# VectorE's order around a block of projections: the short convolution behind the background's taps, and root mean squares computed early

## The chip, the cores and the metric

The kernel runs on one core of a Trainium2 chip. The metric is the device time of one execution in microseconds (us), the median of a few runs. The engines are TensorE (PE in the profile; PEld is its weight load), VectorE (DVE), ScalarE (ACT), GpSimd (POOL) and SyncE (SP), which only issues DMAs here.

## What is computed

One layer of an encoder, for two requests (g = 0 and g = 1) of 2048 tokens with 1024 channels. All weights are shared.

```
h = rmsnorm(x, norm_g);  p = h @ w_in                      # 1024 -> 3328 columns
hy_u, hy_z, cf_a, cf_z, xa_q, xa_z = split(p)
u  = depthwise_conv(hy_u, width 3) -> x0, x1, v
y_hy = x0 * fftconv(v * x1, k2, skip) * silu(hy_z)         # k2: a filter from a small MLP
y_cf = silu(layernorm(depthwise_conv(val * sigmoid(gate), width 31))) * silu(cf_z)
y_xa = attention(xa_q, rmsnorm(mem)) * silu(xa_z)
out  = rmsnorm(x + concat(y_hy, y_cf, y_xa) @ w_out, final_g)
```

## The kernel before

The kernel has three stages. Stage 1 (0 to about 1350 us) makes the projection h @ w_in. Stage 2 (to about 1690 us) runs attention and the frequency side of the long convolution. Stage 3 makes the output projection. The change touches stage 1 only.

In stage 1 the loop goes over the 26 columns of 128 outputs of request 0, then over those of request 1, and in each column over four token tiles `tb` of 512. One column and one token tile are called a **block** here. A block is 24 matmuls of 128x512 (`proj`, L502 to L504) into a PSUM tile `pj`, of which there are two. What follows depends on the column: `x1`, `v` and `x0` are the inputs of the width-3 convolution (`hy_conv`), `z` is a gate that ScalarE writes (L568), `cf` columns feed the width-31 convolution, `q` and `zx` go to attention.

`hy_conv` (L509) takes two tiles of the pool `sm` (six buffers): GpSimd copies the 65 last elements of the tile before (L515), ScalarE copies the PSUM tile (L516, this frees `pj`), GpSimd makes the middle tap (L523), VectorE adds the two others (L525, L527), and in `v` and `x0` columns GpSimd multiplies the result into a 2048-wide tile of the pool `big` (`gate`, L544; three buffers). The finished `big` tile is written to DRAM at the column's end; for `v` columns ScalarE issues that DMA (L558).

Beside the blocks runs **background** work, kept in two queues `fq` and `bgq` of pieces (cost, chain, function). After each block `background(us)` gives a credit of 5.4 us less the block's own VectorE cost (2.2 for x0, x1 and v, 0.8 for cv and q, 0.1 otherwise), and runs pieces until the credit is used. A piece marked as chain runs only when its queue has run nothing yet in that block. The pieces that matter here:

- `cf_background`: the width-31 convolution of one request: four token tiles of 512 tokens, two halves of channels, 30 taps each, each one VectorE instruction (L276, cost 0.9). When both halves are done there follows a chain of five steps: `total` (GpSimd adds, L282), `center` (TensorE means, L286, then VectorE subtracts, L292), `squares`, `var` (L286 again, ScalarE's root, VectorE's reciprocal, L302) and `outp`. The next token tile's first 31 pieces are spread between these steps in five parts.
- `filter_background` (request 1): a three-layer MLP with a sine (L358 on VectorE, L361 and L362 on GpSimd, L364 three times on VectorE, L365), and the filter's taps (L389, L390).
- `kv_background` and `a_background`: keys and values, and the first part of stage 2.

Where request 0 ends, `load_x` loads and normalizes the tokens of request 1 (`normed`): four row tiles of 256 KB per 256 tokens for the sum of squares (L436, ScalarE's L437), and the same tokens transposed in two DMAs of 512 KB (L439) that VectorE scales (L449) by a row that TensorE broadcasts (L447). `build_xt` splits the result into two halves `xh` and `xl` (L468, L469).

The order of each engine's instructions is made by a scheduler when the kernel is built: from the source, it takes what its own timing says is ready. `in_order` binds chosen engines to the source's order: each instruction of a background piece stands behind the one that the source has before it on that engine. It binds TensorE and ScalarE.

Of the kernel before, what the change touches and what calls it, by code (L numbers as in the profile page):

```python
# [18 lines left out]
P = 128  # L19
L = 2048  # L20
D = 1024
# [86 lines left out]
def kernel(ctx: ExitStack, tc: tile.TileContext, a: dict):  # L108
# [77 lines left out]
    def background(us):  # L186

        pace["block"] += 1
        pace["credit"] = min(pace["credit"], us) + us
        chained = set()  # L190
        while pace["credit"] > 0:
            for q in (fq, bgq):
                if not q:
                    continue
                cost, chain, fn = q[0]
                if chain and (id(q) in chained or pace["last"][id(q)] == pace["block"]):
                    continue
                if chain:
                    chained.add(id(q))
                q.popleft()  # L200
                with in_order():
                    fn()
                pace["last"][id(q)] = pace["block"]
                pace["credit"] -= cost
                break
            else:
                break
# [37 lines left out]
    with ExitStack() as c1:  # L245
# [20 lines left out]
        def cf_background(g):  # L266
# [54 lines left out]
            for b in range(NB + 1):  # L321
                first = list(half(sts[b], b, 0)) if b < NB else []
                n = -(-len(first) // 5)
                for i in range(5):
                    bgq.extend(chain[i:i + 1])
                    bgq.extend(first[i * n:(i + 1) * n])
                if b < NB:
                    bgq.extend(half(sts[b], b, 1))
                chain = [(us, True, lambda f=f, b=b: f(sts[b], b)) for us, f in (
                    (0.0, total), (1.4, center), (0.0, squares), (3.4, var), (0.0, outp))]  # L330
# [120 lines left out]

        def load_x(g, tb, mid=None):
            xn = []
            for h in range(2):
                if h and mid:
                    mid()
                xn.append(big().rearrange("p (k t) -> p k t", k=KC))
                normed(xn[h], a["xt"][g, tb, h], xs[g][0, tb * TB + h * 256:tb * TB + (h + 1) * 256, :], 0)
            return xn
# [49 lines left out]
        def hy_conv(st, ps, ch, tb, dst=None):  # L509
# [7 lines left out]
            if tb == NB - 1:  # L517
# [6 lines left out]
                                    op0=ALU.mult, op1=ALU.add)  # L524
            nc.vector.scalar_tensor_tensor(ct[:, o:e], pt[:, o:e], w[0], ct[:, o:e], op0=ALU.mult, op1=ALU.add)  # L525
# [3 lines left out]
            return out, o, e  # L529
# [17 lines left out]
        def hy_u(g, i):  # L547
            st = {}

            def x1(tb, ps):  # L550
                if tb == 0:
                    st["u"] = big()
                hy_conv(st, ps, 4 + i, tb, st["u"])

            def v(tb, ps):
                gate(st["u"], tb, hy_conv(st, ps, 8 + i, tb))
                if tb == NB - 1:
                    nc.scalar.dma_start(UU[i].rearrange("c (n g t) -> c n g t", g=2, t=32)[:, :, g, :],  # L558
                                        st["u"].rearrange("p (n t) -> p n t", t=32))
            return [(COL_X1 + i * P, x1), (COL_V + i * P, v)]  # L560

        def hy_g(g, i):
# [7 lines left out]
            def x0(tb, ps):  # L570
                gate(st["u"], tb, hy_conv(st, ps, i, tb))
                if tb == NB - 1:
                    perm_out(st["u"], GG, i, g)
# [119 lines left out]
        def a_background(n0):  # L693
# [20 lines left out]
            def mult(i):  # L714
# [3 lines left out]
                for s in range(2):  # L718
# [10 lines left out]
        QUEUE = {(0, 0): [kv_background], (0, 4): [lambda: cf_background(0)], (1, 0): [filter_background],  # L729
                 (1, 4): [lambda: cf_background(1)],  # L730
# [31 lines left out]
        for idx, (g, n_, cs) in enumerate(seq):  # L762
            if n_ == 0:
                n = 0
            if True:
# [7 lines left out]
                for tb in range(NB):  # L773
# [3 lines left out]
                    for w, (_, f) in zip(ws, cs):  # L777
                        f(tb, proj(w, tb, 256 if first and tb < HB else TB))
# [333 lines left out]
```

## Time and profile before

| | us |
|---|---|
| median of 3 runs | 2106.33 (2104.52 to 2107.66) |
| profiled execution | 2107.82 |
| its span, first to last instruction | 2106.0 |

The profiled execution is 1.5 us above the median. PE has records for 94% of the span, at a mean granted clock of 0.977 of full speed; DVE is busy for 59%, ACT for 37%, POOL for 40%. In the views "idle before" names what ended an engine's idle time, and `x` counts instructions.

### The profile page before, as it was taken

How to read it: one execution, taken by the hardware profiler on the slowest of the kernel's cores; microseconds unless marked ns; L12 is line 12 of the kernel's file. 1: busy time of each engine (PE TensorE's matmuls, PEld its weight loads, DVE VectorE, ACT ScalarE, POOL GpSimd, SP SyncE). 2: the span in 40 equal slices, each digit the busy share in tenths (PEclk: the TensorE clock that was granted, in tenths of full speed). 3: DMA queues.
4: the chain of work that ended last, by engine and by line, in shares of the span. 5: the costliest groups of instructions: out<-in, count | busy, mean ns of one | idle time of the engine just before them, and what ended most of it. 6: DMA issues, size and time to landing. Idle time of an engine off the chain costs nothing. (4 is left out here: it accounts for less than half of the span.)

```text
span 2106.0 us, 25970 instructions
## 1 busy us (share of the span) xinstructions
PE 1983.5 (94%) x8866; PEld 1500.1 (71%) x8866; DVE 1233.5 (59%) x1779; ACT 780.4 (37%) x1468; POOL 847.8 (40%) x838
## 2 busy tenths in 40 slices
PE   5999989998998999999998999899988899999998
PEld 5887778777887787777776877777533267777776
DVE  4533974959646379445448865278887624344443
ACT  4422112131335244444431222278688622222221
POOL 3332766554543222344434441266598711111110
PEclk8999999999999999999999999999999999999999
DMA  9634134342458323233341325698888685555552
GB/s 333 210 106 158 68 93 116 99 133 80 171 191 278 131 86 108 82 96 84 102 116 56 118 88 189 221 291 263 245 273 273 215 218 135 152 159 148 152 145 61
DMA packets 238558, 328.72 MB, mean 156 GB/s; under 512 B 87177, under 2 KB 117913, under 8 KB 236634
## 3 DMA queue, kind: packets, MB, share of 16 engines
q1 hardware_dynamic: 146026, 260.72, 38.9%
q10 hardware_dynamic: 87056, 54.57, 9.6%
q0 software_dynamic: 5344, 11.77, 2.0%
q8 instruction: 71, 1.16, 0.2%
q14 instruction: 61, 0.50, 0.1%
HBM read 196.37 MB, written 130.61 MB: 155 GB/s over the span
## 5 line engine op out<-in xcount | busy, mean ns | idle before, releaser
L502 PE MATMUL pj<-xh,whi 128*128 128x512 f32 (+1 forms) x1728 | 679.0, 393 | 23.6 <-ACT xh L468 6.7
L503 PE MATMUL pj<-xl,whi 128*128 128x512 f32 (+1 forms) x1728 | 673.4, 390 | 9.7 <-POOL xl L469 9.7
L504 PE MATMUL pj<-xh,wlo 128*128 128x512 f32 (+1 forms) x1728 | 671.8, 389 | 2.0 <-POOL wlo L235 2.0
L276 DVE SCALAR_TENSOR_TENSOR bg<-bg,vb,bg 128x512 f32<-128x512 f32 x480 | 399.0, 877 | 39.6 <-POOL bg L271 35.7
L502 PEld LDWEIGHTS pj<-xh,whi 128*128 128x128 f32 x1728 | 332.3, 193 | 105.2 <-ACT sm L516 15.0
L503 PEld LDWEIGHTS pj<-xl,whi 128*128 128x128 f32 x1728 | 332.8, 193 | 79.7 <-POOL xl L469 11.0
L504 PEld LDWEIGHTS pj<-xh,wlo 128*128 128x128 f32 x1728 | 332.5, 192 | 71.0 <-issue 3.6
L1057 PE MATMUL ms<-wo,mh 128*128 128x512 f32 x512 | 204.3, 399 | 2.2 <-ACT mh L234 2.2
L1058 PE MATMUL ms<-wo,mh 128*128 128x512 f32 x512 | 201.2, 393 | 0.0
L1059 PE MATMUL ms<-wo,ml 128*128 128x512 f32 x512 | 194.3, 397 | 0.2 <-POOL ml L235 0.2
L516 ACT COPY sm<-pj 128x512 f32<-128x512 f32 x96 | 56.5, 589 | 353.4 <-PE pj L504 272.0
L525 DVE SCALAR_TENSOR_TENSOR sm<-sm,va,sm 128x448 f32<-128x448 f32 (+1 forms) x96 | 77.7, 809 | 145.5 <-POOL sm L523 106.0
L544 POOL TENSOR_TENSOR big<-big,sm 128x448 f32<-128x448 f32 (+1 forms) x64 | 121.2, 1894 | 100.9 <-DVE sm L527 100.9
L1060 DVE TENSOR_TENSOR xr<-xr,ms 128x512 f32<-128x512 f32 x64 | 44.0, 688 | 199.0 <-PE ms L1059 198.9
L523 POOL TENSOR_SCALAR sm<-sm,va 128x448 f32<-128x448 f32 (+1 forms) x96 | 110.9, 1155 | 114.3 <-ACT sm L516 110.6
L241 POOL TENSOR_TENSOR ss<-ss,mhalf 128x1 f32<-128x1 f32 x32 | 17.7, 553 | 313.3 <-DVE ss L240 313.3
L1057 PEld LDWEIGHTS ms<-wo,mh 128*128 128x128 f32 x512 | 96.9, 189 | 47.4 <-issue 24.3
L1059 PEld LDWEIGHTS ms<-wo,ml 128*128 128x128 f32 x512 | 96.5, 188 | 21.0 <-DVE mf L1043 0.8
L1058 PEld LDWEIGHTS ms<-wo,mh 128*128 128x128 f32 x512 | 96.9, 189 | 20.0
L239 ACT ACTIVATE junk<-xr 128x1024 bf16<-128x1024 f32 x32 | 33.9, 1060 | 192.4 <-DVE xr L1060 185.9
L925 POOL TENSOR_TENSOR z<-z,us 128x512 f32<-128x512 f32 x64 | 81.9, 1289 | 31.3 <-DVE us L924 22.7
L235 POOL TENSOR_TENSOR wlo<-sm,whi 128x512 fp32r<-128x512 f32 x50 | 75.6, 1526 | 37.2 <-ACT whi L234 28.9
(169 smaller groups left out, 2758.6 us busy)
## 6 DMA issues: line engine op xcount, KB each, us to landing
big<-in_xt_dram SPq DMA_DIRECT2D x32, 512.0 KB, 6.8
in<-x1d SPq DMA_DIRECT2D x128, 128.0 KB, 3.6
aa<-o ACTq DMA_DIRECT2D x64, 256.0 KB, 3.5
at<-aa SPq DMA_DIRECT2D x64, 256.0 KB, 5.0
out_dram<-xr ACTq DMA_DIRECT2D x64, 256.0 KB, 3.8
sm<-in_win_dram SPq DMA_DIRECT2D x52, 256.0 KB, 3.6
ws<-whi SPq DMA_DIRECT2D x52, 256.0 KB, 3.0
ws<-wlo SPq DMA_DIRECT2D x52, 256.0 KB, 4.2
```

The source lines that it names most:

```text
L235: (sub_eng or nc.gpsimd).tensor_tensor(lo, src, hi.bitcast(F32), op=ALU.subtract)
L276: nc.vector.scalar_tensor_tensor(st["a", c], st["h", c][:, k:k + TB], vb[:, 2 * k + c:2 * k + c + 1], st["a", c], op0=ALU.mult, op1=ALU.add)
L502: nc.tensor.matmul(ps[:, ts_], hi, xh[:, k, ts_], start=k == 0, stop=False)
L503: nc.tensor.matmul(ps[:, ts_], hi, xl[:, k, ts_], start=False, stop=False)
L504: nc.tensor.matmul(ps[:, ts_], lo, xh[:, k, ts_], start=False, stop=k == KC - 1)
L523: nc.gpsimd.tensor_scalar(ct[:, o:e], pt[:, o + 1:e + 1], w[1], va[:, 52 + ch:53 + ch], op0=ALU.mult, op1=ALU.add)
L525: nc.vector.scalar_tensor_tensor(ct[:, o:e], pt[:, o:e], w[0], ct[:, o:e], op0=ALU.mult, op1=ALU.add)
L544: nc.gpsimd.tensor_tensor(v, v, out, op=ALU.mult)
L925: nc.gpsimd.tensor_tensor(z, z, us, op=op)
L1057: nc.tensor.matmul(po, mh[:, k, :], woh[k][:, hs], start=i == 0, stop=False)
L1058: nc.tensor.matmul(po, mh[:, k, :], wol[k][:, hs], start=False, stop=False)
L1059: nc.tensor.matmul(po, ml[:, k, :], woh[k][:, hs], start=False, stop=i == 7)
```

## The change

- `in_order` around a background piece binds VectorE too.
- `hy_conv` becomes a generator: up to GpSimd's middle tap it runs where it did; VectorE's two instructions and the gate (`later`) run after the block's background call, bound to VectorE's source order.
- Credit that a block does not use lapses (before, up to one block's worth was kept).
- The chain of `cf_background` has eight steps, three of them empty; the next tile's pieces are spread between them in eight parts.
- The sums of squares of request 1 are made by a background of their own (`squares_background`) during columns v(1) to x1(3) of request 0: eight loads of 1 MB each into `big` tiles, two ScalarE instructions each, the results kept in `rs1`. `load_x` of request 1 (`normed_known`) then has no row loads and no squares.
- Request 1's `cf_background` is queued one column earlier.

```diff
-        pace["credit"] = min(pace["credit"], us) + us
+        pace["credit"] = min(pace["credit"], 0.0) + us
...
-                with in_order():
+                with in_order((nc.tensor, nc.scalar, nc.vector)):
                     fn()
...
-                n = -(-len(first) // 5)
-                for i in range(5):
+                n = -(-len(first) // 8)
+                for i in range(8):
...
-                    (0.0, total), (1.4, center), (0.0, squares), (3.4, var), (0.0, outp))]
+                    (0.0, None), (0.0, total), (1.4, center), (0.0, None), (0.0, squares), (0.0, None), (3.4, var), (0.0, outp))]
...
+        def squares_background():
...
+            def rows_in(i):
+                st[i] = big().rearrange("p (j d) -> p j d", j=2)
+                nc.sync.dma_start(st[i], xs[1][0, i * 256:(i + 1) * 256, :].rearrange("(j p) d -> p j d", p=P))
...
+            def rstd(i):
+                t, ss = st.pop(i), rs1[:, 2 * i:2 * i + 2]
+                for j in range(2):
+                    nc.scalar.activation(t[:, j, :], t[:, j, :], AF.Square, accum_out=ss[:, j:j + 1])
+                nc.vector.tensor_scalar(ss, ss, 1.0 / D / 65536, EPS / 65536, op0=ALU.mult, op1=ALU.add)
+                nc.gpsimd.tensor_tensor(ss, ss, mhalf.broadcast_to([P, 2]), op=ALU.pow)
...
+            for i in range(8):
+                fq.append((0.0, True, lambda i=i: rows_in(i)))
+                fq.append((0.2, True, lambda i=i: rstd(i)))
...
+        def normed_known(xb, src, i):
...
+            for k in range(0, KC, 4):
+                nc.sync.dma_start(xb[:, k:k + 4, :], src[:, k:k + 4, :])
+            dg, r = bt(), ms()[:, 0:256]
+            for t in range(2):
+                dt = dg[:, t * P:(t + 1) * P]
+                nc.vector.tensor_scalar(dt, ident, rs1[:, 2 * i + t:2 * i + t + 1], None, op0=ALU.mult)
+                nc.tensor.matmul(r[:, t * P:(t + 1) * P], ones.bitcast(F32), dt, start=True, stop=True)
...
                                     op0=ALU.mult, op1=ALU.add)
+            yield
             nc.vector.scalar_tensor_tensor(ct[:, o:e], pt[:, o:e], w[0], ct[:, o:e], op0=ALU.mult, op1=ALU.add)
...
             def v(tb, ps):
-                gate(st["u"], tb, hy_conv(st, ps, 8 + i, tb))
-                if tb == NB - 1:
+                cv = hy_conv(st, ps, 8 + i, tb)
+                next(cv)
+
+                def rest():
+                    gate(st["u"], tb, next(cv))
...
-        QUEUE = {(0, 0): [kv_background], (0, 4): [lambda: cf_background(0)], (1, 0): [filter_background],
-                 (1, 4): [lambda: cf_background(1)],
+        QUEUE = {(0, 0): [kv_background], (0, 7): [squares_background], (0, 4): [lambda: cf_background(0)], (1, 0): [filter_background],
+                 (1, 3): [lambda: cf_background(1)],
...
-                    for w, (_, f) in zip(ws, cs):
-                        f(tb, proj(w, tb, 256 if first and tb < HB else TB))
+                    later = [f(tb, proj(w, tb, 256 if first and tb < HB else TB)) for w, (_, f) in zip(ws, cs)]
...
                         background(sum(5.4 - own(col) for col, _ in cs))
+                    with in_order((nc.vector,)):
+                        for f in later:
+                            if f:
+                                f()
```

What this does to VectorE's order is seen at three places. The first is the first x1 column of request 0. Before, 28 taps (L276) stand ahead of the first convolution instruction; the last of them and the first block's convolution (L525, L527; tile `big` is its result) are:

```order
L276 SCALAR_TENSOR_TENSOR bg_2055<-bg_2053,vb,bg_2055 128x512
L525 SCALAR_TENSOR_TENSOR sm_1752<-sm_1749,va,sm_1752 128x448
L276 SCALAR_TENSOR_TENSOR bg_1758<-bg_1756,vb,bg_1758 128x512
L276 SCALAR_TENSOR_TENSOR bg_2419<-bg_2417,vb,bg_2419 128x512
L276 SCALAR_TENSOR_TENSOR bg_2055<-bg_2053,vb,bg_2055 128x512
L527 SCALAR_TENSOR_TENSOR big_1748<-sm_1749,va,sm_1752 128x7x64
L525 SCALAR_TENSOR_TENSOR sm_1800<-sm_1797,va,sm_1800 128x512
L276 SCALAR_TENSOR_TENSOR bg_1758<-bg_1756,vb,bg_1758 128x512
L276 SCALAR_TENSOR_TENSOR bg_2419<-bg_2417,vb,bg_2419 128x512
```

After the change the same column, from its first tap on (L563 and L565 are the convolution now):

```order
L276 SCALAR_TENSOR_TENSOR bg_1757<-bg_1755,vb,bg_1757 128x512 x4
L563 SCALAR_TENSOR_TENSOR sm_1753<-sm_1750,va,sm_1753 128x448
L565 SCALAR_TENSOR_TENSOR big_1749<-sm_1750,va,sm_1753 128x7x64
L276 SCALAR_TENSOR_TENSOR bg_1757<-bg_1755,vb,bg_1757 128x512 x4
L563 SCALAR_TENSOR_TENSOR sm_1797<-sm_1794,va,sm_1797 128x512
L565 SCALAR_TENSOR_TENSOR big_1749<-sm_1794,va,sm_1797 128x8x64
L276 SCALAR_TENSOR_TENSOR bg_1757<-bg_1755,vb,bg_1757 128x512 x3
```

The taps of three half tiles no longer run ahead of the convolution; each block has its three or four taps, then its convolution. The second place is VectorE around the third token tile's `center` (L292) in request 0, before:

```order
L525 SCALAR_TENSOR_TENSOR sm_3690<-sm_3686,va,sm_3690 128x576
L276 SCALAR_TENSOR_TENSOR bg_3451<-bg_3449,vb,bg_3451 128x512
L276 SCALAR_TENSOR_TENSOR bg_3727<-bg_3725,vb,bg_3727 128x512
L527 SCALAR_TENSOR_TENSOR sm_3690<-sm_3686,va,sm_3690 128x576
...
L276 SCALAR_TENSOR_TENSOR bg_3451<-bg_3449,vb,bg_3451 128x512
L276 SCALAR_TENSOR_TENSOR bg_3727<-bg_3725,vb,bg_3727 128x512 x4
L292 TENSOR_TENSOR bg_3163<-bg_3163,ms_3765 128x512
L292 TENSOR_TENSOR bg_3451<-bg_3451,ms_3765 128x512
```

and after:

```order
L276 SCALAR_TENSOR_TENSOR bg_3631<-bg_3629,vb,bg_3631 128x512 x22
L276 SCALAR_TENSOR_TENSOR bg_3899<-bg_3897,vb,bg_3899 128x512 x3
L563 SCALAR_TENSOR_TENSOR sm_3895<-sm_3892,va,sm_3895 128x448
L565 SCALAR_TENSOR_TENSOR sm_3895<-sm_3892,va,sm_3895 128x448
L276 SCALAR_TENSOR_TENSOR bg_3899<-bg_3897,vb,bg_3899 128x512 x4
L563 SCALAR_TENSOR_TENSOR sm_3939<-sm_3936,va,sm_3939 128x512
L565 SCALAR_TENSOR_TENSOR sm_3939<-sm_3936,va,sm_3939 128x512
L292 TENSOR_TENSOR bg_3267<-bg_3267,ms_3991 128x512
L292 TENSOR_TENSOR bg_3631<-bg_3631,ms_3991 128x512
```

Before, the last tap of the half tile that is centered (`bg_3451`) stands four taps ahead of `center`, at the end of a run in which every other tap is one of the next tile (`bg_3727`); after, two convolutions and seven taps of the next tile stand between them. The third place is VectorE in the `x1` and `v` columns of request 1, where the filter's MLP runs beside the blocks. Before, the convolutions of several blocks stand between the filter's steps, and the scheduler fills the gaps:

```order
L358 TENSOR_SCALAR f_6376<-ms_6374,va 128x256
L390 TENSOR_TENSOR f_6371<-ms_6367,f_6371 128x512
L525 SCALAR_TENSOR_TENSOR sm_6363<-sm_6359,va,sm_6363 128x576
L364 SCALAR_TENSOR_TENSOR f_6376<-f_6280,f_6376 128x256
L527 SCALAR_TENSOR_TENSOR big_6209<-sm_6359,va,sm_6363 128x9x64
L364 SCALAR_TENSOR_TENSOR f_6376<-f_6280,f_6376 128x256 x2
```

After, L364 (which waits for GpSimd's L362) stands directly behind L358, and the taps and the convolution behind both:

```order
L390 TENSOR_TENSOR f_7355<-ms_7351,f_7355 128x512
L358 TENSOR_SCALAR f_7362<-ms_7360,va 128x256
L364 SCALAR_TENSOR_TENSOR f_7362<-f_7358,f_7362 128x256 x3
L276 SCALAR_TENSOR_TENSOR bg_6847<-bg_6845,vb,bg_6847 128x512
L563 SCALAR_TENSOR_TENSOR sm_7347<-sm_7343,va,sm_7347 128x576
L565 SCALAR_TENSOR_TENSOR sm_7347<-sm_7343,va,sm_7347 128x576
```

Nothing else can be taken in the time that L364 waits.

## Rows read from the trace of the kernel before

**Rows 1.** Windows of stage 1: length, busy us and (x instructions) by engine, PEclk, DMA.

```profile
260.00:285.00 25.00, 19.03 (x72) 15.18 (x71) 25.00 (x29) 2.81 (x5) 17.15 (x13) 0.86 0.45 105
400.00:420.00 20.00, 15.01 (x58) 11.88 (x57) 20.00 (x23) 2.99 (x4) 9.23 (x6) 0.83 0.34 68
420.00:440.00 20.00, 17.80 (x70) 13.89 (x69) 16.71 (x24) 4.61 (x7) 7.38 (x8) 0.91 0.28 81
440.00:510.00 70.00, 70.00 (x309) 57.57 (x308) 48.17 (x53) 18.23 (x24) 42.51 (x34) 1.00 0.31 107
510.00:540.00 30.00, 23.31 (x88) 17.76 (x87) 23.23 (x29) 7.17 (x10) 10.66 (x10) 0.83 0.30 109
635.00:705.00 70.00, 60.90 (x259) 48.92 (x258) 47.11 (x91) 35.32 (x67) 27.20 (x18) 0.93 0.80 263
705.00:1125.00 420.00, 420.00 (x1874) 330.08 (x1873) 234.26 (x344) 171.94 (x228) 143.10 (x204) 1.00 0.31 92
1125.00:1150.00 25.00, 17.77 (x68) 13.52 (x68) 18.38 (x26) 4.72 (x6) 6.80 (x7) 0.86 0.24 79
1210.00:1235.00 25.00, 20.12 (x76) 15.17 (x75) 15.51 (x18) 4.96 (x7) 7.31 (x4) 0.86 0.23 81
```

**Rows 2.** Waits of PE, 200 to 1345 us: us in total, times, longest.

```profile
PE ms L286 <- POOL bg L282: 21.0, 4, 7.2
PE pj L502 <- ACT sm L516: 6.6, 2, 6.0
PE ms L447 <- DVE bg L446: 5.3, 2, 3.8
PE pj L502 <- ACT big L568: 5.0, 1, 5.0
PE pj L502 <- DVE sm L610: 3.8, 3, 2.4
```

**Rows 3.** Timeline of DVE, 505 to 530 us: start, us, line, count.

```profile
506.40 21.55 DVE L276 SCALAR_TENSOR_TENSOR bg<-bg,vb,bg 128x512 f32<-128x512 f32 x25
```

**Rows 4.** Timelines of ACT and POOL, 246 to 276 us.

```profile
271.47 0.60 ACTq L558 DMA_DIRECT2D uu<-big  x1
272.19 0.59 ACT L516 COPY sm<-pj 128x512 f32<-128x512 f32 x1 [15.45 <-POOL sm L515]
...
269.29 2.16 POOL L544 TENSOR_TENSOR big<-big,sm 128x576 f32<-128x576 f32 x1 [3.40 <-DVE sm L527]
```

**Rows 5.** Costliest groups of DVE, 200 to 640 us: busy, mean ns, idle before.

```profile
L276 DVE SCALAR_TENSOR_TENSOR bg<-bg,vb,bg 128x512 f32<-128x512 f32 x233 | 203.4, 922 | 18.8 <-POOL bg L271 16.8 <-POOL sm L513 0.7
L525 DVE SCALAR_TENSOR_TENSOR sm<-sm,va,sm 128x512 f32<-128x512 f32 (+2 forms) x48 | 41.8, 871 | 72.4 <-POOL sm L523 56.1 <-POOL sm L513 16.3
L527 DVE SCALAR_TENSOR_TENSOR sm<-sm,va,sm 128x512 f32<-128x512 f32 (+2 forms) x32 | 31.1, 971 | 0.6
L527 DVE SCALAR_TENSOR_TENSOR big<-sm,va,sm 128x512 f32<-128x512 f32 (+2 forms) x16 | 22.4, 1399 | 0.2
```

**Rows 6.** Costliest groups of POOL on the page, whole span.

```profile
L544 POOL TENSOR_TENSOR big<-big,sm 128x448 f32<-128x448 f32 (+1 forms) x64 | 121.2, 1894 | 100.9 <-DVE sm L527 100.9
L523 POOL TENSOR_SCALAR sm<-sm,va 128x448 f32<-128x448 f32 (+1 forms) x96 | 110.9, 1155 | 114.3 <-ACT sm L516 110.6
```

**Rows 7.** The group of ACT nearest to the new squares, whole span.

```profile
L239 ACT ACTIVATE junk<-xr 128x1024 bf16<-128x1024 f32 x32 | 33.9, 1060 | 192.4 <-DVE xr L1060 185.9 <-DMA xr<-in_x_prompt_dram 6.3 <-DMA g<-gg 0.2
```

**Rows 8.** DMA issues on the page: KB each, median us to landing.

```profile
big<-in_xt_dram SPq DMA_DIRECT2D x32, 512.0 KB, 6.8
```

**Rows 9.** Groups of DVE beside the filter, 900 to 1100 us.

```profile
L364 DVE SCALAR_TENSOR_TENSOR f<-f,f 128x256 f32<-128x256 f32 x33 | 18.8, 570 | 11.4 <-POOL f L362 10.7
L390 DVE TENSOR_TENSOR f<-ms,f 128x512 f32<-128x512 f32 x18 | 12.4, 691 | 37.5 <-ACT f L389 36.9 <-PE ms L387 0.5
L358 DVE TENSOR_SCALAR f<-ms,va 128x256 f32<-128x256 f32 x11 | 5.9, 536 | 5.3 <-PE ms L356 5.3
```

**Rows 10.** The tap's group on DVE at 226 to 248 us, then at 248 to 282 us.

```profile
L276 DVE SCALAR_TENSOR_TENSOR bg<-bg,vb,bg 128x512 f32<-128x512 f32 x22 | 16.2, 786 | 0.0
L276 DVE SCALAR_TENSOR_TENSOR bg<-bg,vb,bg 128x512 f32<-128x512 f32 x25 | 26.2, 1097 | 0.0
```

**Rows 11.** Window of the column v(0).

```profile
226.00:248.00 22.00, 22.00 (x98) 18.09 (x97) 20.98 (x30) 3.40 (x6) 12.42 (x9) 1.00 0.13 48
```

More of the change, by code (lines that the diff above doesn't have):

```diff
@@ L328, in cf_background @@
                     bgq.extend(half(sts[b], b, 1))
-                chain = [(us, True, lambda f=f, b=b: f(sts[b], b)) for us, f in (
-                    (0.0, total), (1.4, center), (0.0, squares), (3.4, var), (0.0, outp))]
+                chain = [(us, True, lambda f=f, b=b: f and f(sts[b], b)) for us, f in (
+                    (0.0, None), (0.0, total), (1.4, center), (0.0, None), (0.0, squares), (0.0, None), (3.4, var), (0.0, outp))]
         def filter_background():
@@ L450, in normed @@
                                                op0=ALU.mult, op1=ALU.mult)
+        rs1 = const.tile([P, 16], F32, name="rs1")
+        def squares_background():
+            st = {}
+            def rows_in(i):
[18 more added lines that the diff above has]
+                nc.tensor.matmul(r[:, t * P:(t + 1) * P], ones.bitcast(F32), dt, start=True, stop=True)
+            for k in range(KC):
+                nc.vector.scalar_tensor_tensor(xb[:, k, :], xb[:, k, :], va[:, k:k + 1], r,
+                                               op0=ALU.mult, op1=ALU.mult)
         def load_x(g, tb, mid=None):
@@ L457, in load_x @@
                 xn.append(big().rearrange("p (k t) -> p k t", k=KC))
-                normed(xn[h], a["xt"][g, tb, h], xs[g][0, tb * TB + h * 256:tb * TB + (h + 1) * 256, :], 0)
+                if g:
+                    normed_known(xn[h], a["xt"][g, tb, h], 2 * tb + h)
+                else:
+                    normed(xn[h], a["xt"][g, tb, h], xs[g][0, tb * TB + h * 256:tb * TB + (h + 1) * 256, :], 0)
             return xn
@@ L528, in hy_conv @@
                                            op0=ALU.mult, op1=ALU.add)
-            return out, o, e
+            yield out, o, e
         def scatter(pm, tok, n):
@@ L552, in x1 @@
                     st["u"] = big()
-                hy_conv(st, ps, 4 + i, tb, st["u"])
+                cv = hy_conv(st, ps, 4 + i, tb, st["u"])
+                next(cv)
+                return lambda: next(cv)
             def v(tb, ps):
-                gate(st["u"], tb, hy_conv(st, ps, 8 + i, tb))
-                if tb == NB - 1:
+                cv = hy_conv(st, ps, 8 + i, tb)
+                next(cv)
+                def rest():
+                    gate(st["u"], tb, next(cv))
+                    if tb < NB - 1:
+                        return
                     nc.scalar.dma_start(UU[i].rearrange("c (n g t) -> c n g t", g=2, t=32)[:, :, g, :],
                                         st["u"].rearrange("p (n t) -> p n t", t=32))
+                return rest
             return [(COL_X1 + i * P, x1), (COL_V + i * P, v)]
@@ L570, in x0, with rest @@
             def x0(tb, ps):
-                gate(st["u"], tb, hy_conv(st, ps, i, tb))
-                if tb == NB - 1:
-                    perm_out(st["u"], GG, i, g)
+                cv = hy_conv(st, ps, i, tb)
+                next(cv)
+                def rest():
+                    gate(st["u"], tb, next(cv))
+                    if tb == NB - 1:
+                        perm_out(st["u"], GG, i, g)
+                return rest
             return [(COL_ZH + i * P, z), (COL_X0 + i * P, x0)]
```

## The prediction

> **What bounds the kernel now.** I read the busy shares first: TensorE has work for 94% of the span, so only time in which it stands still, or runs at its lower clock, can be won. The windows of stage 1 say where that is. In 440 to 510 us nothing disturbs it: 309 matmuls in 70 us, 4.41 a us, so a block of 24 takes 5.44 us. From 705 to 1125 us, beside the filter, it is busy for 420.00 of 420 us [rows 1]. Between 200 and 1345 us seven stretches fall short. Counted in matmuls that are missing at 4.41 a us they lose: 260 to 285 us, 25 - 72/4.41 = 8.7 us; 400 to 420, 6.9; 420 to 440, 4.1; 510 to 540, 10.1; 635 to 705, 11.3; 1125 to 1150, 9.6; 1210 to 1235, 7.8; together 58.5 us [rows 1]. That is more than the waits themselves, because behind a wait the granted clock is the lower of its two levels for a while (0.83 to 0.93 in the mean of these windows; 1.2 instead of 2.4 GHz while it lasts).
>
> The waits of TensorE name three causes. Four times a mean (L286) waits for GpSimd's total, 21.0 us [rows 2]; these are the stretches at 420, 510, 1125 and 1210, 31.6 us with the clock. The timeline at 506 us shows why: VectorE runs 25 taps in one go, 21.55 us [rows 3], every other one for the next token tile, and the last tap of the tile that is wanted is late. Twice the projection waits for its PSUM tile (ScalarE's L516 and L568) for 5 to 6 us [rows 2]: the stretches at 260 and 400, 15.6 us. At 272 us ScalarE's copy has waited 15.45 us; it is put down to GpSimd's tail copy, but just ahead of it ScalarE issued the DMA that waits for the gate, and the gate waited for VectorE's convolution [rows 4], which stood behind taps. The third is the passage to request 1 (635 to 705, 11.3 us): L447 and L502 wait for VectorE [rows 2], which waits for sums of squares while the DMA engines are busy for 0.80 of the time [rows 1].
>
> **The order.** From the pacing rules alone a conv block gets 3.2 of credit, 3.55 taps of 0.9; a gate column's block up to six. Bound to the source VectorE then does 3.55 taps and one convolution per block: 3.55 x 0.92 + 0.87 + 0.97 or 1.40 = 5.1 to 5.5 us [rows 5], 5.25 in the mean over the columns, against 5.44. So it keeps up, with little to spare. A convolution now waits behind its block's taps (3.3 us). In that time ScalarE's copy and GpSimd's middle tap (1.16 us, [rows 6]) are done, so their wait is covered; I let it end 4 to 8 us after the block. What is queued behind it is GpSimd's gate (1.89), the next block's middle tap (1.16) and then ScalarE's copy [rows 6], some 4.4 us in all. TensorE needs the PSUM tile of that copy 16.3 us (three blocks) after the first block's end, so the convolution may be up to 12 us late. If VectorE is slower than 5.44 us a block this cover is eaten up, and then TensorE goes at VectorE's rate. I leave 3 of the 15.6 us (bounds 0, and 32 by the second rival).
>
> **Empty steps and lapsing credit.** With an empty step after the last tap, `total` comes at least two blocks behind that tap and `center` a block later; with VectorE in order nothing can hold that tap back. I take the four waits as gone: -31.6 us. The lower bound is the first rival's. The rules still fit all pieces into the blocks: the last step of request 1 falls into its last column, as does the first part of stage 2; the empty steps cost nothing, and the fourth token tile's last steps of request 0 move into request 1's first column, where VectorE has little else.
>
> **Root mean squares.** At the passage 32 loads of 256 KB and 32 squares go. The 1 MB per 256 tokens of transposed loads, the scaling and the splitting stay, and so does their chain through three `big` tiles, with VectorE's L610 (which frees a PSUM tile) between them. Halved traffic shortens that chain, it does not remove it: I leave 4 of 11.3 us (bounds 0 and 11.3). The squares return as 16 ScalarE instructions in conv columns. The nearest row is 1.06 us for 1024 elements [rows 7], so 2.1 us and two accumulator reads in every second block, where ScalarE is busy for 3.40 of 22 us [rows 11]. Behind them stands the next copy of a PSUM tile, so the loads matter: 1 MB each on SP's queue, one block ahead. 512 KB take 6.8 us in the median [rows 8]; for 1 MB that bounds it by 6.8 and 13.6 us. Up to 6.8 it is covered by the block between; at 13.6 each would be late by about 3, 24 us in all. As the columns have a DMA share of 0.13 [rows 11] and that median was taken mostly at high shares, I take the low end and leave 1 us. VectorE's small instruction behind the squares holds the block's taps back by some 3 us, which the 12 us above cover.
>
> **Beside the filter.** L364 now stands directly behind L358 and waits for GpSimd with nothing to fill in: about 1 us per MLP step by the idle time that the row shows (11.4 us for 33) [rows 9]. Per two blocks VectorE then has 0.54 + 3 x 0.57 + 1.0 + 0.9 for L390 [rows 9], 3.5 taps (by the pacing rules) at 0.92 and two convolutions of 2.0 [rows 5]: 11.4 us, against 10.9 us for two blocks of projections alone, to which the filter's own matmuls are added. It fits; 0 us (at most 0.5 x 16 steps = 8).
>
> **The sum.** Against the profiled execution, 2107.8: -58.5 + 3 + 4 + 1 = -50.5, so 2057.3. That execution was 1.5 us above the median, so the forecast is **2056 us**. Stage 2 and 3 have the same instructions, and stage 3 the same order; in stage 2 the scheduler's order differs in places, for which I have no row and allow 5 us either way.
>
> **Rivals.**
> First, *the convolution's waits come back*: the means no longer wait, but `pj` does, as often as before, and the passage is unchanged. Then 2107.8 - 31.6 - 1.5 = 2075 us. For it: those waits come through GpSimd's order, which is not bound. Against: VectorE's surplus of taps, 28 ahead of the first convolution, is what started them. 10%.
>
> Second, *VectorE becomes the bound in conv columns*. Two neighbouring stretches show what is open: a tap takes 786 ns at 226 us and 1097 ns at 248 us [rows 10]. At 1.10 a conv block takes 5.7 to 6.2 us, 0.5 over TensorE's 5.44; for 64 conv blocks (those beside the filter have more time) +32 us: 2088. For it: VectorE was busy for 20.98 of 22 us in v(0) already; against: that column ran 22 taps and its convolutions beside 12.42 us of GpSimd, and TensorE lost nothing [rows 11]. 16%. The Trainium skill's page "SBUF — State Buffer", section "Who interferes with whom", speaks for this rival: a VectorE instruction with two inputs in SBUF (taps and convolutions are such) and a GpSimd instruction that reads SBUF exclude each other for the whole of one of them. By that rule the slower tap would hold in all conv columns and the time would be this rival's. The trace agrees only in part: in v(0) the busy times of both add up to 33.4 us in 22.
>
> Third, on the other side, *VectorE's fixed order adds waits that nothing fills*. Before, the convolution found its middle tap unfinished for 72.4 us over 48 blocks, 1.5 us each [rows 5]. If that wait stays in full behind the taps, a conv block takes 5.25 + 1.5 = 6.8 us, 1.3 over; 64 blocks cost 85 us, and 2056 + 85 = 2141. It decides from 6.2 us a block on (50.5 us over 64 blocks). Against it: the taps in front last longer than the copy and the middle tap. 6%.
>
> **The numbers.** Forecast 66%, rivals 10, 16 and 6%, and 2% that gains and new waits cancel. All seven losses gone would be 2048; what lies outside the seven stretches and stage 2 may add up to 10 more: low end 2038. The high end, 2086, takes in the first rival and most of the second. Measurements of this kernel can tell about 0.2%, 4 us. Faster 91%, within 3%, slower 6%.
>
> **What would show it.** Right: no wait of a mean for L282; windows of conv columns with 4.4 matmuls a us and clock 1.00; taps in groups of three or four between convolutions; less than half the DMA traffic at the passage. Wrong: VectorE without idle time in conv columns while TensorE waits for L516 (second rival); VectorE idle for the middle tap or the squares (third); ScalarE waiting for the 1 MB loads.

## The result, and the profile after

The changed kernel takes 2070.79 us in the median of four runs (2066.19 to 2073.04); the kernel before, measured beside it, 2105.74 us. The ratio is 0.9834, with a 95% interval of 0.9821 to 0.9848. The forecast was 2056, the range 2038 to 2086: the sign and the range held, and 35 of the 50 us came. The profiled execution took 2071.46 us, with a span of 2069.7.

The waits of TensorE in stage 1 of the changed kernel (us in total, times, longest), to be set beside [rows 2]:

```profile
PE pj L539 <- DVE sm L661: 7.0, 2, 4.8
PE pj L539 <- ACT big L614: 6.1, 2, 5.0
PE ms L231 <- DVE bg L235: 2.2, 1, 2.2
PE ms L405 <- DVE f L390: 2.0, 1, 2.0
...
PE ms L481 <- DVE bg L480: 0.5, 1, 0.5
```

No mean (L286) waits for GpSimd's total any more, and the passage's wait (L481, which was L447) is 0.5 instead of 5.3 us. What is left are two kinds of wait for a projection's PSUM tile (L661 and L614, 13.1 us), at other places than in [rows 2], and two smaller waits outside the projections: L405 for the filter's L390, and L231, in the first part of stage 2, for VectorE's L235. The windows say where, in the columns of [rows 1]:

```profile
430.00:500.00 70.00, 70.00 (x309) 57.62 (x308) 55.42 (x52) 20.28 (x26) 38.03 (x30) 1.00 0.35 121
385.00:410.00 25.00, 20.03 (x78) 16.03 (x77) 24.26 (x26) 4.14 (x5) 9.22 (x7) 0.86 0.52 123
580.00:612.00 32.00, 27.21 (x114) 21.89 (x113) 23.21 (x29) 4.00 (x7) 9.21 (x6) 0.89 0.69 225
640.00:680.00 40.00, 37.24 (x167) 30.17 (x166) 25.60 (x46) 16.95 (x21) 15.82 (x9) 1.00 0.64 202
700.00:1030.00 330.00, 330.00 (x1473) 256.22 (x1472) 202.42 (x287) 151.28 (x203) 127.15 (x182) 1.00 0.31 97
1040.00:1060.00 20.00, 16.84 (x60) 11.17 (x59) 17.27 (x23) 8.89 (x9) 3.37 (x2) 0.83 0.50 108
1225.00:1245.00 20.00, 17.75 (x77) 13.03 (x76) 18.76 (x24) 4.26 (x8) 3.42 (x2) 0.91 0.52 176
```

The undisturbed window still holds 309 matmuls in 70 us. Counted as in the prediction, 7.3 us are missing at 385 us, 6.1 at 580, 2.1 at 640, 6.4 at 1040 and 2.5 at 1225: 24 us, where 58.5 were missing before. Two of the places, 385 and 1040, are the passage from a v column to a z column. ScalarE at the first of them, in the changed kernel:

```profile
377.57 0.59 ACT L553 COPY sm<-pj 128x512 f32<-128x512 f32 x1 [1.51 <-PE pj L541]
382.96 1.15 ACT L614 ACTIVATE big<-pj 128x512 f32<-128x512 f32 x1 [4.80 <-PE pj L541]
397.10 0.52 ACTq L603 DMA_DIRECT2D uu<-big  x1
397.66 1.06 ACT L614 ACTIVATE big<-pj 128x512 f32<-128x512 f32 x1 [13.55 <-POOL big L582]
```

The last block of v ended at 377.5 us. The DMA of uu was issued 19.6 us later, when the gate (L582) was done, and the Silu copy of the z column that stood behind it in ScalarE's queue had waited 13.55 us. VectorE and GpSimd say why the gate was late:

```profile
375.84 6.25 DVE L276 SCALAR_TENSOR_TENSOR bg<-bg,vb,bg 128x512 f32<-128x512 f32 x4
382.02 0.74 DVE L563 SCALAR_TENSOR_TENSOR sm<-sm,va,sm 128x512 f32<-128x512 f32 x1
382.79 0.75 DVE L565 SCALAR_TENSOR_TENSOR sm<-sm,va,sm 128x512 f32<-128x512 f32 x1
383.46 4.03 DVE L276 SCALAR_TENSOR_TENSOR bg<-bg,vb,bg 128x512 f32<-128x512 f32 x3
```

```profile
383.63 2.08 POOL L582 TENSOR_TENSOR big<-big,sm 128x512 f32<-128x512 f32 x1 [1.39 <-DVE sm L565]
...
394.88 2.19 POOL L582 TENSOR_TENSOR big<-big,sm 128x576 f32<-128x576 f32 x1 [3.75 <-DVE sm L565]
```

Three taps beside one gate and the next block's middle tap take 4.03 us, 1.34 each, and the convolution that the last gate waits for ends 17 us after its block.

At 1040 us the DMA of uu waited for the gate as well (8.77 us), but there VectorE had stood idle ahead of the last convolution of the column. Its next tap waited for the first tap of a new half tile, which GpSimd makes (L271), and the convolution is bound behind that tap:

```profile
1038.60 0.75 DVE L276 SCALAR_TENSOR_TENSOR bg<-bg,vb,bg 128x512 f32<-128x512 f32 x1 [5.48 <-POOL bg L271]
```

Of TensorE's waits at 1040 us, 1.1 us are for L614 and 2.0 us for L390. The one at 1225 us is L231's, whose L235 stood behind six taps of VectorE (6.5 us). The third place, 580 us, is the q column, whose PSUM tile VectorE reads itself (L661), behind 22 taps in one go:

```profile
579.58 20.56 DVE L276 SCALAR_TENSOR_TENSOR bg<-bg,vb,bg 128x512 f32<-128x512 f32 x22
600.05 0.68 DVE L661 SCALAR_TENSOR_TENSOR sm<-pj,sm 128x512 fp32r<-128x512 f32 x1
```

The tap's group between 200 and 640 us, for [rows 5]:

```profile
L276 DVE SCALAR_TENSOR_TENSOR bg<-bg,vb,bg 128x512 f32<-128x512 f32 x239 | 256.7, 1075 | 16.0 <-POOL sm L555 6.9 <-POOL bg L271 2.6
```

A tap takes 1.075 us there, not the 0.92 of the forecast.

### The profile page after: what moved, and what is told of

Its sections match the earlier page's. It is cut to its first block, busy times and chain, and to the rows that moved or that the text cites. A ratio compares the mean times of both kernels' runs of the same rounds, so it can differ in the third digit from the quotient of the medians.

```text
span 2069.7 us, 25885 instructions
## 1 busy us (share of the span) xinstructions
PE 1974.5 (95%) x8866; PEld 1495.1 (72%) x8866; DVE 1306.3 (63%) x1771; ACT 779.1 (38%) x1439; POOL 851.8 (41%) x838
## 4 chain that ended last, share of the span: by engine, by line
PE 68%; DVE 11%; DMA 8%; issue 6%; POOL 5%; ACT 3%; SPq 1%; ACTq 0%; POOLq 0%; DVEq 0%
PE pj L539 12%; PE pj L540 12%; PE pj L541 12%; PE ms L1111 5%; PE ms L1112 5%; PE ms L1113 5%; DVE bg L276 5%; PE tr L924 2%; PE tr L1088 1%; PE po L931 1%; DMA in<-xf 1%; PE ms L909 1%; DMA aa<-o 1%; DMA big<-in_xt_dram 1%; PE ms L697 1%
## 5 line engine op out<-in xcount | busy, mean ns | idle before, releaser
L276 DVE SCALAR_TENSOR_TENSOR bg<-bg,vb,bg 128x512 f32<-128x512 f32 x480 | 473.0, 986 | 37.0 <-POOL bg L271 17.2
L553 ACT COPY sm<-pj 128x512 f32<-128x512 f32 x96 | 56.5, 589 | 362.3 <-PE pj L541 294.3
L582 POOL TENSOR_TENSOR big<-big,sm 128x448 f32<-128x448 f32 (+1 forms) x64 | 124.5, 1946 | 96.6 <-DVE sm L565 89.6
L560 POOL TENSOR_SCALAR sm<-sm,va 128x448 f32<-128x448 f32 (+1 forms) x96 | 111.9, 1166 | 114.7 <-ACT sm L553 102.7
L1112 PEld LDWEIGHTS ms<-wo,mh 128*128 128x128 f32 x512 | 96.6, 189 | 19.9
L563 DVE SCALAR_TENSOR_TENSOR sm<-sm,va,sm 128x448 f32<-128x448 f32 (+1 forms) x96 | 85.3, 889 | 9.5 <-POOL sm L560 8.1
L614 ACT ACTIVATE big<-pj 128x512 f32<-128x512 f32 x32 | 36.2, 1130 | 133.3 <-PE pj L541 119.8
```

The source lines that it names most:

```text
L276: nc.vector.scalar_tensor_tensor(st["a", c], st["h", c][:, k:k + TB], vb[:, 2 * k + c:2 * k + c + 1], st["a", c], op0=ALU.mult, op1=ALU.add)
L553: nc.scalar.copy(pt[:, 65:577], ps)
L560: nc.gpsimd.tensor_scalar(ct[:, o:e], pt[:, o + 1:e + 1], w[1], va[:, 52 + ch:53 + ch], op0=ALU.mult, op1=ALU.add)
L582: nc.gpsimd.tensor_tensor(v, v, out, op=ALU.mult)
L1112: nc.tensor.matmul(po, mh[:, k, :], wol[k][:, hs], start=False, stop=False)
```

## Experiments

Every time is a median. The kernel before, measured beside them, gave 2106.4 us with the first four kernels, 2106.3 with the second four and 2107.6 with the last four.

### The parts of the change alone

**Order alone**: VectorE bound behind its source order in the background, and the short convolution behind a block's taps.

```diff
-                with in_order():
+                with in_order((nc.tensor, nc.scalar, nc.vector)):
...
+                    with in_order((nc.vector,)):
+                        for f in later:
...
```

> The kernel before, with VectorE bound to source order and the short convolution behind a block's taps, and nothing else of the change. My theory: the taps that VectorE ran ahead made the total late, so the order alone shortens the four waits of a mean (L286) to 2 us or less each and takes 25 to 31 us off the 2105.7; the passage to request 1 stays (11 us) and the waits for a projection's PSUM tile stay about as long as in the changed kernel (17 us lost): 2075 to 2083 us. Rival: without empty steps the total still stands directly behind the last tap and the mean one block behind it, so that half or more of the four waits stays: 2088 us or more.

Measured: 2084.42 us, ratio 0.9901 [0.9887, 0.9916], 22 us saved, between the bounds of theory and rival. Of the four waits for the total one is left:

```profile
PE ms L286 <- POOL bg L282: 4.2, 1, 4.2
```

So the order alone takes three of the four waits away, and one needs something else.

**Empty steps and lapsing credit alone**, with request 1's taps queued a column earlier, as in the change.

```diff
-        pace["credit"] = min(pace["credit"], us) + us
+        pace["credit"] = min(pace["credit"], 0.0) + us
...
-                    (0.0, total), (1.4, center), (0.0, squares), (3.4, var), (0.0, outp))]
+                    (0.0, None), (0.0, total), (1.4, center), (0.0, None), (0.0, squares), (0.0, None), (3.4, var), (0.0, outp))]
...
-                 (1, 4): [lambda: cf_background(1)],
+                 (1, 3): [lambda: cf_background(1)],
```

> The kernel before with the empty steps (eight parts, earlier second queue entry) and the lapsing credit alone; VectorE's order stays free. If the order is what matters, taps of the next tile still run ahead and the total is late by as much as the scheduler lets it be: 2092 to 2106 us. Rival: two blocks (10.9 us) more between last tap and total, and one more before the mean, cover waits of 5 us each whatever the order, so either part alone is enough: 2074 to 2086 us.

Measured: 2160.97 us, ratio 1.0252 [1.0237, 1.0267]. Theory and rival both missed by over 50 us. TensorE's waits in stage 1:

```profile
PE ms L447 <- DVE bg L446: 30.1, 3, 14.4
PE ms L286 <- POOL bg L282: 24.4, 4, 8.9
```

The second line is the point that was asked: all four waits stay. VectorE's timeline at the place of [rows 3] shows that, unbound, it fills the added room with more taps, 35 in one go where it had 25:

```profile
504.88 26.96 DVE L276 SCALAR_TENSOR_TENSOR bg<-bg,vb,bg 128x512 f32<-128x512 f32 x35
```

The first line was 5.3 us before [rows 2]. Behind the passage to request 1 ScalarE's sums of squares wait for their loads, 41.3 us in 16 waits between 680 and 765 us. ScalarE in that stretch:

```profile
699.46 0.63 ACT L437 ACTIVATE bg<-bg 128x512 f32<-128x512 f32 x1 [2.30 <-DMA bg<-in_x_sample_dram]
...
703.68 0.63 ACT L437 ACTIVATE bg<-bg 128x512 f32<-128x512 f32 x1 [2.56 <-DMA bg<-in_x_sample_dram]
...
707.67 0.63 ACT L437 ACTIVATE bg<-bg 128x512 f32<-128x512 f32 x1 [3.26 <-DMA bg<-in_x_sample_dram]
...
735.99 1.14 ACT L296 ACTIVATE bg<-bg 128x512 f32<-128x512 f32 x2
```

They come one at a time, 4 us apart, while the last token tile's chain is still under way (its squares, L296, stand at 736 us). That chain holds four of the six `bg` tiles into which these loads go. The DMA queue's own waits agree: a load (L436) is issued only when the square of an earlier one (L437) has set its tile free. From 640 to 770 us in this kernel, and below it from 615 to 705 us in the kernel before:

```profile
SPq L436 <- ACT bg L437: 48.9, 19, 5.3
SPq L436 <- ACT bg L437: 12.2, 10, 2.8
```

**Early root mean squares alone.**

```diff
...
+                if g:
+                    normed_known(xn[h], a["xt"][g, tb, h], 2 * tb + h)
...
```

> The kernel before with the early root mean squares alone. My forecast for this part: the passage to request 1 loses 4 instead of 11.3 us and the squares cost 1 us elsewhere: 2099 us (2096 to 2102). Rival: the passage is set by the transposed loads and the three big tiles, which stay: 2104 to 2107 us.

Measured: 2108.36 us, ratio 1.0005 [0.9994, 1.0016]: nothing. The windows of this kernel, at the squares' columns and at the passage, and below them those of the kernel before:

```profile
290.00:340.00 50.00, 44.37 (x185) 35.32 (x184) 19.11 (x26) 16.16 (x30) 26.83 (x34) 0.97 0.54 163
620.00:700.00 80.00, 77.00 (x352) 62.91 (x351) 46.75 (x89) 25.91 (x34) 27.85 (x16) 1.00 0.68 219
```

```profile
290.00:340.00 50.00, 49.39 (x217) 40.17 (x216) 25.51 (x27) 9.37 (x17) 30.17 (x34) 1.00 0.36 101
620.00:700.00 80.00, 70.90 (x308) 57.53 (x307) 48.39 (x99) 38.59 (x81) 26.27 (x19) 0.94 0.79 256
```

At the passage 44 matmuls more fit, 10 us. At 290 us 32 fewer do, 7 us: TensorE waits there for weights (7.0 us), whose casts stand behind the squares on ScalarE. So nothing was gained, as the rival said (its range ended at 2107), but not for its reason: the passage did get shorter.

**Everything but the empty steps, the lapse and the earlier start of request 1's taps**, and **everything but the squares**, two more parts of the same change:

> The changed kernel without the empty steps and without the lapsing credit (five parts, second queue entry where it was before): order and early root mean squares together. The order alone gave 2084.4; the early squares took some 10 us off the passage to request 1 and gave them back elsewhere while VectorE's order was free. Theory: with the order bound the squares cost nothing, so that they add about 10 us, and the means keep one wait (4 us, some 7 with the clock), which is what the empty steps are worth: 2073 to 2079 us. Rival 1: the empty steps are worth nothing once the order is bound: 2068 to 2072 us. Rival 2: the squares give nothing here either: 2081 to 2086 us.

Measured: 2083.75 us, ratio 0.9896 [0.988, 0.9912], inside the second rival: in time the squares give nothing beside the order either. Three waits for the total are there:

```profile
PE ms L286 <- POOL bg L282: 11.7, 3, 6.0
```

Yet the passage is shorter here too. The same window in the order alone and, below it, in this kernel:

```profile
620.00:700.00 80.00, 69.67 (x300) 56.27 (x299) 52.38 (x98) 37.95 (x71) 29.63 (x19) 0.94 0.76 244
620.00:700.00 80.00, 76.55 (x349) 62.47 (x348) 44.65 (x83) 26.99 (x34) 25.35 (x14) 1.00 0.63 194
```

The 49 matmuls more, 11 us, are lost again elsewhere: the waits for the total grew from 4.2 to 11.7 us, and those for the copy of a PSUM tile (L553, which was L516) from 1.4 to 7.1.

> The changed kernel without the early root mean squares: order, empty steps and lapsing credit. The empty steps alone lost 45 us in the columns behind the passage to request 1, where the last token tile's steps held bg tiles that the sums of squares needed. Theory: that clash comes with the longer chain of steps and not with the free order, so that it is here too and the early squares, worth nothing alone, are what removes it: 2095 us or more. Rival: the clash came from the free order: 2070 to 2082 us.

Measured: 2129.57 us, ratio 1.0104 [1.0088, 1.012]: the theory held. The waits for the total are gone, and the clash behind the passage is there as in the empty steps alone:

```profile
PE ms L447 <- DVE bg L446: 30.9, 4, 14.4
```

So the parts don't add up. With order and squares the empty steps and the lapse, with the earlier start of request 1's taps, give 13 us (2083.75 to 2070.79); with the order alone they lose 45 (2084.42 to 2129.57); the squares, worth nothing without them, are worth 59 with them.

**Unused credit kept**, the changed kernel without the lapse:

> The changed kernel with unused credit carried over to the next block as before. Theory: blocks behind a chain step then get up to seven or more taps, VectorE's backlog grows, and the waits for it with that: 2074 to 2082 us. Rival: the lapsing of credit matters little, since few blocks leave credit unused: 2068 to 2073 us.

Measured: 2081.54 us, ratio 0.9874 [0.9855, 0.9893], 10.8 us more than the changed kernel; the theory held, if not by VectorE's backlog alone. Two waits for the total are back (7.9 us), and one of 6.4 us for a subtraction of GpSimd (L235). So most of the 13 us needs the lapse, which I had given no price of its own. The lapse without the empty steps was not run.

### The waits that are left

**The uu DMA later.** In the changed kernel, ScalarE issues it three blocks later; ScalarE's order is bound there too.

```diff
-                    nc.scalar.dma_start(UU[i].rearrange("c (n g t) -> c n g t", g=2, t=32)[:, :, g, :],
+                        late.extend((None, None, lambda: nc.scalar.dma_start(
+                            UU[i].rearrange("c (n g t) -> c n g t", g=2, t=32)[:, :, g, :],
...
+                    with in_order((nc.vector, nc.scalar)):
+                        later.append(late.popleft() if late else None)
...
```

> The changed kernel with ScalarE's issue of the uu DMA three blocks later (16 us) in its queue, so that the Silu copies of the next column no longer stand behind it while it waits for the gate. Theory: the two stalls at the passage from v to z (7.6 and 7.9 us lost) come from that issue alone: 2070.8 - 15.5 = 2055 us (2053 to 2059). Rival: VectorE is late whatever ScalarE does, and the wait moves to the next copy that needs a tile from it: 2066 to 2071 us.

Measured: 2059.2 us, ratio 0.9779 [0.9759, 0.98], 11.6 us less than the changed kernel. No copy L614 is waited for any more, so the issue was what carried VectorE's lateness to TensorE. Of the 15.5 us expected 11.6 came, 0.2 us short of the theory's range; the wait for L390, beside the filter, grew from 2.0 to 3.4 us:

```profile
PE pj L539 <- DVE sm L661: 6.8, 2, 4.8
PE ms L405 <- DVE f L390: 3.4, 1, 3.4
```

**A slower pace**, without and with the later DMA.

```diff
-                    yield 0.9, False, lambda k=k: tap(st, c, k)
+                    yield 1.0, False, lambda k=k: tap(st, c, k)
...
-            return OWN.get(base, 0.1)
+            return OWN.get(base, 0.5)
...
-                 (1, 3): [lambda: cf_background(1)],
+                 (1, 1): [lambda: cf_background(1)],
```

> The changed kernel with fewer taps per block: a tap is charged 1.0 instead of 0.9, the columns without a convolution 0.5 more, and request 1's taps start two columns earlier so that all of them still fit. Theory: VectorE's backlog (taps of 0.99 us on average, not 0.92) is the common cause of the stalls at v to z (7.6 and 7.9 us lost) and in the q column (8.9 us): all go, 2045 to 2052 us. Rival: the stalls at v to z are due to the wait of ScalarE's DMA issue whatever the pace, and only the q column's goes: 2059 to 2064 us.

> The slower pace together with the uu DMA issued three blocks later. The later issue alone gave 2059.2. Theory: what is left there is the q column's stall (8.9 us) and smaller waits for VectorE of 2 to 4 us, all from its backlog: 2044 to 2050 us, and no better than the slower pace alone by more than 2 us. Rival: the lower pace leaves steps that come too late or collide beside the filter: 2055 us or more.

Measured: 2066.3 us (0.9804 [0.9787, 0.9822]) and 2061.36 us (0.9797 [0.9779, 0.9814]). By time the theory fell in both; the rival's number came in the second alone. In stage 1 the slower pace without the later DMA did what the theory says: the waits at 385, 580 and 1040 us are gone, though a tap still takes 1.071 us there; 3.9 us are left of L661's. But the first wait of stage 2 in this kernel, 1.6 us in the changed kernel, is now:

```profile
PE ms L909 <- DMA wo<-qs: 13.0, 1, 13.0
```

Its GpSimd timeline shows what is ahead of that load:

```profile
1302.50 1.27 POOL L311 TENSOR_TENSOR bg<-bg,bg 128x512 f32<-128x512 f32 x1 [2.25 <-DMA bg<-sz]
1303.71 1.19 POOL L874 DMA_DIRECT2D wo<-kb  x2
1304.89 0.55 POOL L876 DMA_DIRECT2D wo<-vt  x1
1305.43 1.44 POOL L885 DMA_DIRECT2D wo<-qs  x2
```

With fewer taps a block the last output step (L311) comes behind the third of the last column's four blocks, not behind the first, and GpSimd issues stage 2's first loads in order behind it. In the changed kernel it issued them 9 us before TensorE ended stage 1, here 1 us after. TensorE ended stage 1 at 1302 us and stood still until 1315.

**The gate on VectorE**, with the later DMA and alone.

```diff
-            nc.gpsimd.tensor_tensor(v, v, out, op=ALU.mult)
+            nc.vector.tensor_tensor(v, v, out, op=ALU.mult)
```

> The changed kernel with the later uu DMA and with the gate (a product of two operands in SBUF) computed by VectorE instead of GpSimd, so that taps no longer run beside it. The trace of the changed kernel shows taps of 0.74 us where GpSimd does nothing and of 1.42 us where most of the tap lies beside the gate. Theory: the mean tap falls from 0.99 to 0.80 to 0.85 us, which pays for the 64 gates of about 1.1 us on VectorE: 2056 to 2062 us, against 2059.2. Rival: the tap is slow for another reason and stays above 0.95 us; then VectorE takes 1.1 us more in each gate block and becomes the bound in those columns: 2080 us or more.

> The changed kernel with the gate on VectorE and nothing else. Theory: taps that run beside the gate on GpSimd are the root of VectorE's backlog, and ScalarE's DMA issue at v to z waits for the gate only because of it; then the later issue adds nothing: 2046 to 2050 us. Rival: the two causes add up, and without the later issue half or more of the 11.6 us that it gave is missing: 2054 us or more.

Measured: 2047.77 us (0.972 [0.9699, 0.974]) and 2053.68 us (0.9747 [0.9728, 0.9766]). Groups of VectorE in the first of them, 200 to 640 us:

```profile
L276 DVE SCALAR_TENSOR_TENSOR bg<-bg,vb,bg 128x512 f32<-128x512 f32 x239 | 219.6, 920 | 13.9 <-POOL sm L555 4.9 <-POOL bg L271 2.5
L582 DVE TENSOR_TENSOR big<-big,sm 128x512 f32<-128x512 f32 (+2 forms) x32 | 42.2, 1317 | 1.1
```

The tap fell from 1.075 us in the changed kernel to 0.920 there, and from 0.986 to 0.860 over the whole span. That was a little less than expected and did not pay in full for the gates: VectorE is busy for 1329.9 us, and for 1310.0 with the later DMA alone. Still the kernel is 11.4 us faster than with the later DMA alone, better than expected, and TensorE's waits at 580, 1040 and 1225 us are gone. That the gate, behind the convolution on the same engine, waits for no other engine is the likely reason; no run shows it by itself. The three taps of the block shown above, in this kernel:

```profile
382.00 2.31 DVE L276 SCALAR_TENSOR_TENSOR bg<-bg,vb,bg 128x512 f32<-128x512 f32 x3
```

At the passage this kernel loses more than the changed one, 8.3 us for 2.1:

```profile
640.00:680.00 40.00, 34.92 (x140) 27.67 (x139) 18.50 (x27) 15.24 (x19) 10.67 (x8) 0.91 0.52 156
```

The gate alone falls between theory and rival: 5.9 of the later DMA's 11.6 us are missing. The two causes overlap by half.

**And the q column off VectorE.** ScalarE scales the tile into SBUF, rounds it there, and GpSimd subtracts.

```diff
-                nc.scalar.activation(qh, ps, AF.Copy, scale=0.125)
-                nc.vector.scalar_tensor_tensor(ql, ps, 0.125, qh.bitcast(F32), op0=ALU.mult, op1=ALU.subtract)
+                nc.scalar.activation(ql.bitcast(F32), ps, AF.Copy, scale=0.125); nc.scalar.copy(qh, ql.bitcast(F32))
+                nc.gpsimd.tensor_tensor(ql, ql.bitcast(F32), qh.bitcast(F32), op=ALU.subtract)
```

> The gate on VectorE and the later uu DMA (2047.8 together), and in the q columns VectorE's instruction that reads the projection's PSUM tile replaced by a second ScalarE instruction and a GpSimd subtraction in SBUF, so that the tile no longer waits for VectorE. What is left in stage 1 there is one stall of 5.1 us (block 13.0 instead of 5.4 us) at the passage, where that instruction stands behind VectorE's scaling, which waits for the transposed loads. Theory: that block loses nothing more, 2047.8 - 7.6 = 2040 us (2038 to 2044). Rival: the next thing that waits for the loads takes its place: 2046 to 2049 us.

Measured: 2061.37 us, ratio 0.978 [0.9763, 0.9797], 13.6 us worse than without it, and worse than theory and rival. TensorE's waits:

```profile
PE tr L224 <- DMA u<-uu: 7.1, 1, 7.1
PE pj L539 <- DMA whi<-ws: 5.2, 1, 5.2
PE ms L909 <- DMA wo<-qs: 4.7, 1, 4.7
```

At the passage it went as the rival says: the weights, loaded on the same queue as the transposed inputs, take the PSUM tile's place, and 640 to 680 us hold 139 matmuls where they held 140. The loss itself lies behind stage 1, which TensorE even ended 1 us earlier: at the start of stage 2 it waits 7.1 us for the load of u and 4.7 for wo, where it waited 1.9 and 2.2. Why these loads are later here is not shown. The fastest kernel is the one with the gate on VectorE and the later DMA: 2047.77 us.

## Why the prediction was right, and what it mis-sized

**The means, -31.6: right.** All four waits are gone. But the reason given, that an empty step alone puts the total two blocks behind its tap, was only half of it. It needs the bound order, as the prediction said; unbound, the waits grew. And the bound order with the empty steps, but with the credit kept, left two waits; the order alone left one, order and squares three. The lapse, to which the prediction gave no price of its own, carries most of the 13 us.

**The waits for the PSUM tile, 15.6 leaving 3: this is the term that failed.** The windows at 385, 580, 1040 and 1225 us lose 7.3 + 6.1 + 6.4 + 2.5 = 22.3 us. The first two are waits for a PSUM tile; 1040 is one in part, and 1225 is none, but VectorE is late at each. With 22.3 for 3, and 2.1 for the passage's 4, the sum of the prediction comes to 2057.3 + 19.3 - 1.9 = 2074.7 on its own scale; 2071.5 was profiled. Four things were wrong in it.

First, the tap: 0.92 us was the mean under the free order. Behind a block's taps the convolution's gate falls beside the next block's taps, and there they take longer. By start and duration of each in the trace, 299 of the changed kernel's 480 taps start while GpSimd computes nothing; they take 0.75 us in the mean. Of the 50 that start while a gate runs, 48 end 0.53 to 0.56 us after the gate's end, and take 1.95 us in the mean; of the 55 that start while a middle tap (L560) runs, 46 end likewise, 1.12 us. So the slow taps are taps that were held. In the kernel before, 22 were held by a gate and 27 by a middle tap. With 1.075 for 0.92 a conv block of the prediction is 5.25 + 3.55 x 0.155 = 5.8 us, over TensorE's 5.44, and VectorE falls behind by 0.36 us a block.

Second, the cover of 12 us counted only what stands behind the convolution on GpSimd. At the end of a v column ScalarE's DMA issue waits for the gate as well, and the next column's copies stand behind it. The prediction had read just this at 272 us in the kernel before, and left it out of the sum; the later DMA showed that this alone was worth 11.6 us.

Third, the q column was not in the sum: its PSUM tile is read by VectorE itself, so that every tap of its backlog stands in the way.

Fourth, the bound order can hold the convolution behind a tap that waits for GpSimd, as at 1040 us (5.48 us for L271). The sum had no such wait; the third rival had one.

**The second rival had the right mechanism and the wrong extent.** Taps slowed by GpSimd did eat the cover, but at a few places, not in 64 blocks at VectorE's rate: from 275 to 380 us, nearly all in x1 and v columns, VectorE was busy for 98 of 105 us, and 463 matmuls ran, 4.41 a us, so TensorE lost nothing. The Trainium skill's page "SBUF — State Buffer", section "Who interferes with whom", says that a VectorE instruction with two inputs in SBUF and a GpSimd instruction that reads SBUF exclude each other. The trace agrees: a tap that starts beside a gate ends 0.53 to 0.56 us after it in 48 of 50 cases. The prediction's row against this, busy times of both that add up to 33.4 us in 22, does not speak against it, because a held instruction's row contains its wait: in the changed kernel a tap that starts at 384.24 us takes 2.02 us, beside a gate that ends at 385.71.

**The passage, 11.3 leaving 4, and the squares, +1: right in the sum**, 2.1 us were left, and from 275 to 380 us, where the squares run, TensorE is busy throughout. But the DMA traffic at the passage is not under half, as the prediction wanted for a sign: 202 GB/s from 640 to 680 us against 263 [rows 1]. And the parts are not separate. Alone the squares lost at 290 us what they won at the passage, and their real work in this change is another: they free the `bg` tiles that the longer chain needs at the passage. The prediction let the last steps of request 0 "move into request 1's first column, where VectorE has little else"; without the early squares that move costs 59 us. It priced the engine and not the tiles.

**The filter, 0: nearly right; the end: right.** TensorE is busy throughout from 700 to 1030 us, but at 1049 us it waits 2.0 us for the filter's L390. It ended stage 1 at 1358.7 us before the change and at 1320.3 after, 38.4 us earlier; 2 us of that are lost behind stage 1, within the 5 that were allowed. The first rival's time, 2075, was nearer than the forecast, but its reason was not quite the measured one: the passage did improve. The third rival's 85 us didn't come, but its mechanism, VectorE idle in its fixed order, is what stands at 1040 us.

What stays open is why the waits for the total grow when the squares are added to the order without empty steps; no run splits that. That the clash at the passage comes through the `bg` tiles rests on the waits of the loads for them (48.9 us where the kernel before had 12.2) and on its absence with the squares; a kernel with more such tiles was not tried.

## What to carry to other kernels

A duration taken as a mean belongs to the order in which it was measured: when a change moves an instruction beside another engine's work, look for rows of that neighbourhood. When an engine is allowed to be late by so much, walk every queue in which something waits for it, DMA issues among them, and every tile that is held meanwhile. Parts of a change that look separate can need each other, so measure them together and one taken away, not only one alone.

## What the runs showed of the hardware

Work moved onto the busier engine made the kernel faster. With the later DMA in both, 64 gates on VectorE (1.36 us each, 86.8 in all) in place of GpSimd (1.95 each) cost only 19.9 us of VectorE's time, because its 480 taps fell from 0.995 to 0.860 us in the mean, 64.9 us in all; the kernel won 11.4 us.

A tap that starts while GpSimd runs a gate is not slowed by a share but held to the gate's end: 48 of 50 ended 0.53 to 0.56 us after it, against 0.75 us for a whole tap with GpSimd idle.
